# Reordering the input projection's groups in a hybrid decoder trunk, and the sampled convolution as products of all taps

## The chip, the core and the metric

The kernel runs on one core of a Trainium2 chip. The engines named below are TensorE (PE, the matrix engine, with its weight loads), VectorE (DVE), ScalarE (ACT), GpSimd (POOL) and SyncE (SP, which issues most DMAs). Each engine works through its own instruction stream in order and waits on semaphores for the others. The metric is the device time of one execution, in microseconds.

## The reference

A trunk of two layers processes two batches at once: a prompt of 512 tokens, and 8 sampled sequences of 4 tokens each with a paged cache of 2048 earlier positions. Each layer projects 1024 features to 2048, gives them to four mixers of width 256, joins these by an output projection, and ends with a gated feed-forward part. Cut to what the change touches:

```python
h = rms_norm(x, g_mix_pre)
a, ga, u, vb, q, k, v, xd = split(h @ w_in, 8)              # eight groups of 256 columns
# A: causal depthwise convolution, 31 taps; the sampled batch has 30 earlier rows in state_conv
ext = concatenate([prev, a * sigmoid(ga)], axis=1)
ya = silu(layer_norm(conv_general_dilated(ext, w_dw, feature_group_count=256) + b_dw))
# B: chunked spatial gating
v_ = layer_norm(gelu(vb));  yb = gelu(u) * (einsum('gts,bnsgc->bntgc', tril(w_s), v_) + b_s)
# C: differential attention, 4 heads with two softmax maps each;  yc = rms_norm(o, 1e-5) * (1 - lam_init)
# D: causal pooling over 2/4/8/16 rows, minus the token, per-group linear
mix = concatenate([ya, yb, yc, yd], axis=-1) @ w_out
x = x + rms_norm(mix, g_mix_post)
x = x + rms_norm((silu(gate) * up) @ w_down, g_ffn_post)    # gate, up = rms_norm(x, g_ffn_pre) @ w_gu
```

## The kernel before

Features lie on the partitions and tokens along the free axis. Dense products are made as three: each operand is split into a rounded part and a rest (`hi`, `lo`), and hi·hi, lo·hi and hi·lo are summed in PSUM. `whi` and `wlo` are the split weights; the rounding (line 194) is done on ACT, the difference (line 197) on DVE or POOL.

**The input projection.** The list `order` names eight groups of 256 columns: 0 (a), 256 (its gate), 1280 (k), 1024 (q), 1536 (v), 1792 (pooling), 512 (u) and 768 (vb). Each of the groups but v is worked in two blocks of 128 columns; each block first makes a half of 256 columns (tokens 0 to 255) and, two steps later, a half of 288 (the other 256 and the 32 sampled tokens). A half is 24 matmuls into a tile of the pool `acc`, which has two banks of PSUM, given out in program order. ACT copies the results out (lines 374 to 377).

**The flows.** Mixers are Python generators. The loop over steps calls `advance`, which lets each active flow issue one more piece, so that a mixer's instructions are put between the projection's. A flow in `urgent` issues under a high priority. `conv` (31 taps on DVE, then transposes, LayerNorm and tanh), `attention`, `gating` and `pooling` become active when their columns are there; a scheduler then orders each engine's stream by readiness and priority.

**Attention** works in units (i, hh) of a block of 128 queries and a head, for heads 0 and 1 (c = 0) and then 2 and 3 (c = 1). `scores` makes two score tiles `s`, a reduction with bias and minimum on DVE (line 501) and an exp on ACT (line 503); `weights` takes a reciprocal, combines the two maps (lines 513 to 515), transposes (line 518) and copies to `pt` (line 520); `values` fills `oT`. After the last unit the tail (lines 543 to 560) takes squares (`sq`), a power on POOL (line 554), its broadcast `rb`, and makes `yc`.

**Gating** transposes the 128x128 weights `wn` into `wt` (lines 578 to 581), multiplies them with `sgr`, applies gelu to all four parts of `uv` and the sampled columns of `zs` (lines 593, 594), makes `vn` and, at lines 612 and 615, `yb`.

**The output projection** (`project_last`) runs over `W_OUT_TURNS`, four token tiles in two halves each; each turn sums 24 matmuls in the order of `W_OUT_ORDER`, whose entries 0 and 1 are ya, 2 and 3 yb, 4 and 5 yc, 6 and 7 yd. After both halves of a tile `finish` adds the residual, normalizes twice (lines 1300 to 1315, on DVE, ACT and POOL) and turns the result back with PE transposes (`sx`, line 239), which `xlo` and `xhi` (lines 241, 242) split for the feed-forward part.

**The sampled mixers** (`sample`) run beside the output projection. `sample_conv` holds, for 8 sequences, 30 earlier rows and 4 new ones in `ext` (tile `scx`) and adds 31 taps on DVE: two operations at line 883 and sixty at line 886, all 128x32. The sampled attention follows; POOL gathers its pages (`kr`, line 1000).

Of the kernel before, what the change touches and what calls it, by code (L numbers as in the profile page):

```python
# [24 lines left out]
CW = 31  # L25
# [19 lines left out]
W_OUT_ORDER = (6, 7, 0, 1, 2, 3, 4, 5)  # L45
# [77 lines left out]
def trunk(ctx, tc, A, O):  # L123
# [18 lines left out]
    def ps():  # L142
        return psx("ps")
# [210 lines left out]
    def mixing(l, mp, early):  # L354
# [35 lines left out]
        def ev_qk(nm, c, f):  # L390
# [20 lines left out]
            (1536, "v"),  # L411
            (1792, [(14, ev_copy(dext[0], 14, 1.0, 15)), (15, ev_copy(dext[1], 15, 1.0, 15))]),
            (512, [(4, ev_copy(uv[:, 0], 4)), (5, ev_copy(uv[:, 1], 5))]),
            (768, [(6, ev_copy(uv[:, 2], 6)), (7, ev_copy(uv[:, 3], 7))]),
# [17 lines left out]
        convs = []  # L432

        def conv():
            for c in range(2):
                while len(convs) <= c:
                    yield
                yield from convs[c]
            o = ps()
# [128 lines left out]
        def gating():  # L568
# [23 lines left out]
            for f in (2, 0):  # L592
                S.activation(uv[:, f:f + 2], uv[:, f:f + 2], AF.Gelu)
            S.activation(zs[:, 4:8, :], zs[:, 4:8, :], AF.Gelu)
# [10 lines left out]
            for c in range(2):  # L605
                o = acc()
                for n in range(4):
                    for hh in range(2):
# [4 lines left out]
                                       bsg[:, c:c + 1, :].to_broadcast([128, 4, 128]), op0=ALU.mult, op1=ALU.add)  # L613
                tf = uv[:, 2 + c, :]
# [104 lines left out]
        for u in range(n + LAG):  # L719
# [19 lines left out]
            if b >= 0:  # L739
# [9 lines left out]
                if c0 == 256 and i == 0:  # L749
                    convs.append(taps(0))  # L750
                    active.append(conv())
                if c0 == 256 and i == 1:
                    convs.append(taps(1))
# [7 lines left out]
                if i == "v":  # L761
                    done.add("v")
                if c0 == 768 and i == 1:
                    active.append(gating())
                    urgent.append(active[-1])
# [90 lines left out]
    def sample_conv(l, mp, cmn):  # L856
# [25 lines left out]
        for c in range(2):  # L882
            V.tensor_scalar(a[:, c], ext[:, c, :, 0:4], pf[:, 8 + c:9 + c], pf[:, c:c + 1], op0=ALU.mult, op1=ALU.add)
        for t in range(1, CW):
            for c in range(2):
                V.scalar_tensor_tensor(a[:, c], ext[:, c, :, t:t + 4], pf[:, 8 + 2 * t + c:9 + 2 * t + c], a[:, c],  # L886
                                       op0=ALU.mult, op1=ALU.add)
            if t % 4 == 0:
                yield
        o = ps()  # L890
# [18 lines left out]
    def sample(l, sp, share):  # L909
        ys = sp.tile([128, 8, NT], F32, tag="ys", name="ys")  # L910
        hs_in = sp.tile([128, 8, NT], F32, name="hs_in")
        with tc.tile_pool(name=f"smx{l}", bufs=1, reuse_waits="tile") as mp:
            yield
            flows = [sample_conv(l, mp, sp), sample_gate(l, mp, sp), sample_pool(l, mp, sp, PW[l])]
            while flows:
                for fl in list(flows):
                    if next(fl, 0) == 0:
                        flows.remove(fl)
                yield
# [555 lines left out]
```

## Time and profile before

| | |
|---|---|
| median of 3 runs | 1471.88 us (1468.3 to 1475.19) |
| the profiled execution | 1470.1 us |
| its span, first to last instruction | 1468.2 us |
| PE busy | 1393.0 us, 95% |
| DVE, ACT, POOL busy | 816.3, 490.4, 253.9 us |
| mean granted TensorE clock | 0.981 |
| instructions | 22964 |

Busy times come from one profiled execution. The granted clock is the share of full speed that TensorE was given: 1.00 is 2.4 GHz, 0.50 is 1.2 GHz, and a figure between them is a stretch that had both. Matmuls are pipelined, so rows of 0.29 us can start every 0.13 us. What ended an engine's idle time is inferred from semaphore events.

### The profile page before, as it was taken

To read this page: it belongs to the slowest core of one execution; us is meant where nothing else is said; L and a number is where in the kernel's file an instruction comes from. 1 tells how busy PE (TensorE), PEld (TensorE's weight loads), DVE (VectorE), ACT (ScalarE), POOL (GpSimd) and SP (SyncE) were. 2 spreads that over 40 slices of the span, in tenths; PEclk is the share of its full clock that TensorE was granted. 3 is DMA by queue.
4 is the path that set the end of the run, shared out by engine and by line. 5 is a ranking of instruction groups with operands and counts; after the bars stand their busy time and mean duration, and the time that the engine had idled before them with its cause. 6 is when DMAs were issued, how large, how long until landed. Compare 5 with 4: busy or idle time off the path is not lost.

```text
span 1468.2 us, 22964 instructions
## 1 busy us (share of the span) xinstructions
PE 1393.0 (95%) x9274; PEld 1085.7 (74%) x9274; DVE 816.3 (56%) x1624; ACT 490.4 (33%) x972; POOL 253.9 (17%) x271
## 2 busy tenths in 40 slices
PE   6999798989999999999989997989899999999997
PEld 6988677856676777777779886787566677777775
DVE  4997577866424323433669856867564333333344
ACT  4345444322224221222333464433222332222231
POOL 1000245443300000000210004434342000000003
PEclk9999998999999999999999999999999999999999
DMA  6220336786859731323432213378767596213132
GB/s 206 93 87 30 131 117 213 257 299 230 286 177 292 238 137 58 104 69 128 152 115 73 73 53 109 128 244 299 274 235 266 182 299 210 100 58 115 58 133 90
DMA packets 155204, 235.60 MB, mean 160 GB/s; under 512 B 8880, under 2 KB 116410, under 8 KB 155098
## 3 DMA queue, kind: packets, MB, share of 16 engines
q1 hardware_dynamic: 136522, 166.76, 34.8%
q0 software_dynamic: 18432, 67.12, 12.8%
q8 instruction: 73, 1.20, 0.3%
q14 instruction: 33, 0.27, 0.1%
q10 hardware_dynamic: 144, 0.26, 0.0%
HBM read 222.07 MB, written 12.04 MB: 159 GB/s over the span
## 4 chain that ended last, share of the span: by engine, by line
PE 73%; DVE 8%; issue 7%; DMA 6%; POOL 3%; ACT 2%; another core or an unknown queue 0%; SPq 0%; POOLq 0%; DVEq 0%; ACTq 0%
PE acc L128 57%; PE sx L128 8%; DMA kr<-in_cache_k_dram,ik 4%; PE ps L128 2%; PE s L128 2%; DVE sca L886 2%; POOL vr L1030 1%; DVE wlo L197 1%; PE oT L128 1%; POOL kr L1000 1%; DVE m L1315 1%; ACT whi L194 1%; POOL rsw L178 1%; DMA rws<-in_w_gu_dram 1%; PE ps L518 1%
## 5 line engine op out<-in xcount | busy, mean ns | idle before, releaser
L128 PE MATMUL acc<-xhi,whi 128*128 128x512 f32 (+2 forms) x1152 | 409.5, 357 | 3.7 <-issue 1.7
L128 PE MATMUL acc<-xlo,whi 128*128 128x512 f32 (+2 forms) x1152 | 406.7, 353 | 4.2 <-DVE xlo L242 3.2
L128 PE MATMUL acc<-xhi,wlo 128*128 128x512 f32 (+2 forms) x1152 | 407.1, 354 | 0.4 <-issue 0.2
L197 DVE TENSOR_TENSOR wlo<-raw,whi 128x1024 fp32r<-128x1024 f32 x172 | 216.6, 1265 | 198.8 <-ACT whi L194 193.0
L194 ACT CAST whi<-raw 128x1024 fp32r<-128x1024 f32 x178 | 184.3, 1048 | 362.9 <-PE acc L128 320.8
L128 PEld LDWEIGHTS acc<-xhi,whi 128*128 128x128 f32 x1152 | 219.7, 191 | 47.5 <-issue 14.2
L128 PEld LDWEIGHTS acc<-xlo,whi 128*128 128x128 f32 x1152 | 219.9, 191 | 35.8 <-issue 5.7
L128 PEld LDWEIGHTS acc<-xhi,wlo 128*128 128x128 f32 x1152 | 219.6, 191 | 34.6 <-issue 7.9
L128 PE MATMUL acc<-whi,h 128*128 128x512 f32 x704 | 224.7, 396 | 0.6 <-issue 0.6
L128 PEld LDWEIGHTS acc<-whi,h 128*128 128x128 f32 x704 | 131.3, 188 | 44.5 <-issue 11.2
L128 PE MATMUL acc<-wlo,h 128*128 128x512 f32 x352 | 138.4, 395 | 0.0
L1290 POOL TENSOR_TENSOR m<-m,g_g_ffn_post 128x512 f32<-128x512 f32 x14 | 20.2, 1449 | 511.2 <-ACT junk L1289 511.2
L1003 DVE STREAM_TRANSPOSE kt<-kr 128x1024 f32<-128x1024 f32 x64 | 78.3, 1234 | 47.4 <-DMA kr<-in_cache_k_dram,ik 26.9
L1000 POOL DMA_INDIRECT kr<-in_cache_k_dram,ik x64 | 70.3, 1099 | 109.8 <-DVE kt L1003 85.3
L427 DVE SCALAR_TENSOR_TENSOR cacc<-hext,pf,cacc 128x512 f32<-128x512 f32 x120 | 86.9, 745 | 0.8
L128 PEld LDWEIGHTS acc<-wlo,h 128*128 128x128 f32 x352 | 66.1, 188 | 18.0 <-issue 4.6
L1030 POOL DMA_INDIRECT vr<-in_cache_v_dram,iv x64 | 60.5, 945 | 84.7 <-PE sx L128 67.0
L1359 DVE SCALAR_TENSOR_TENSOR th<-th,acc 128x512 f32<-128x512 f32 (+1 forms) x46 | 29.6, 644 | 78.9 <-PE acc L128 78.9
L178 POOL TENSOR_TENSOR rsw<-rsw,mhalf 128x1 f32<-128x1 f32 (+2 forms) x62 | 38.5, 628 | 172.0 <-DVE rsw L177 169.1
L128 PE MATMUL sx<-kt,qs 128*32 128x128 f32 x1024 | 49.3, 278 | 9.3 <-issue 8.6
L554 POOL TENSOR_TENSOR rse<-e,mhalf 128x8 f32<-128x8 f32 x4 | 7.5, 1879 | 257.4 <-DVE e L552 257.4
L1361 ACT CAST h<-th 128x512 fp32r<-128x512 f32 (+1 forms) x48 | 27.9, 582 | 66.5 <-DVE th L1359 58.9
(422 smaller groups left out, 1835.9 us busy)
## 6 DMA issues: line engine op xcount, KB each, us to landing
raw<-in_w_gu_dram SPq DMA_DIRECT2D x44, 1024.0 KB
raw<-in_w_down_dram SPq DMA_DIRECT2D x20, 1024.0 KB
rws<-in_w_gu_dram SPq DMA_DIRECT2D x40, 512.0 KB
raw<-in_w_in_dram SPq DMA_DIRECT2D x16, 1024.0 KB
raw<-in_w_out_dram SPq DMA_DIRECT2D x8, 1024.0 KB
rwo<-in_w_out_dram SPq DMA_DIRECT2D x16, 512.0 KB
rws<-in_w_down_dram SPq DMA_DIRECT2D x16, 512.0 KB
x<-x_t SPq DMA_DIRECT2D x12, 512.0 KB
```

The source lines that it names most:

```text
L128: T.matmul(out, lhsT, rhs, start=start, stop=stop)
L178: G.tensor_tensor(y, v, mhalf[:P, :n], op=ALU.pow)
L194: S.copy(hi, src)
L197: eng.tensor_tensor(lo, src, hi.bitcast(F32), op=ALU.subtract)
L427: V.scalar_tensor_tensor(a, hext[c][:, t:t + SEQ], pf[:, 8 + 2 * t + c:9 + 2 * t + c], a, op0=ALU.mult, op1=ALU.add)
L886: V.scalar_tensor_tensor(a[:, c], ext[:, c, :, t:t + 4], pf[:, 8 + 2 * t + c:9 + 2 * t + c], a[:, c], op0=ALU.mult, op1=ALU.add)
L1000: G.indirect_dma_start(out=kr, out_offset=None, in_=ck, in_offset=bass.IndirectOffsetOnAxis(ap=ik[:, s, bg:bg + 1], axis=0))
L1003: V.transpose(kt, kr)
L1030: G.indirect_dma_start(out=v.rearrange("p t e -> p (t e)"), out_offset=None, in_=cv, in_offset=bass.IndirectOffsetOnAxis(ap=iv[:, s, a:a + ...
L1290: (V if (t, half) == (3, 1) else G).tensor_tensor(m[t][:, hs], m[t][:, hs], gain[:, hs], op=ALU.mult)
L1359: V.scalar_tensor_tensor(th[:, :n], th[:, :n], 0.5, ou[:, :n], op0=ALU.mult, op1=ALU.mult)
L1361: S.copy(hh, th[:, :n])
```

## The change

Five edits, as the diff shows. In the input projection vb comes before the pooling columns and u. The gelu is split: the half for vb is issued early, the half for u when u is done; the flow of the gating starts after vb. The order of the output projection's parts is yc, ya, yd, yb. The convolution's flow becomes urgent after its taps. The sampled convolution makes, for each half of the channels and of the sequences, one product of all 31 taps (4 sequences x 4 tokens x 31) and one sum over the taps; the bias is added afterwards. The three sampled flows issue under the high priority.

```diff
-W_OUT_ORDER = (6, 7, 0, 1, 2, 3, 4, 5)
+W_OUT_ORDER = (4, 5, 0, 1, 6, 7, 2, 3)
...
             (1536, "v"),
+            (768, [(6, ev_copy(uv[:, 2], 6)), (7, ev_copy(uv[:, 3], 7))]),
             (1792, [(14, ev_copy(dext[0], 14, 1.0, 15)), (15, ev_copy(dext[1], 15, 1.0, 15))]),
             (512, [(4, ev_copy(uv[:, 0], 4)), (5, ev_copy(uv[:, 1], 5))]),
-            (768, [(6, ev_copy(uv[:, 2], 6)), (7, ev_copy(uv[:, 3], 7))]),
...
                 yield from convs[c]
+            urgent.append(flow["conv"])
+            yield
...
-            for f in (2, 0):
-                S.activation(uv[:, f:f + 2], uv[:, f:f + 2], AF.Gelu)
-            S.activation(zs[:, 4:8, :], zs[:, 4:8, :], AF.Gelu)
+            S.activation(uv[:, 2:4], uv[:, 2:4], AF.Gelu)
+            S.activation(zs[:, 6:8, :], zs[:, 6:8, :], AF.Gelu)
...
+                yield
+            while "u" not in done:
+                yield
+            S.activation(uv[:, 0:2], uv[:, 0:2], AF.Gelu)
+            S.activation(zs[:, 4:6, :], zs[:, 4:6, :], AF.Gelu)
+            for c in range(2):
                 tf = uv[:, 2 + c, :]
...
+                if c0 == 512 and i == 1:
+                    done.add("u")
...
         for c in range(2):
-            V.tensor_scalar(a[:, c], ext[:, c, :, 0:4], pf[:, 8 + c:9 + c], pf[:, c:c + 1], op0=ALU.mult, op1=ALU.add)
-        for t in range(1, CW):
-            for c in range(2):
-                V.scalar_tensor_tensor(a[:, c], ext[:, c, :, t:t + 4], pf[:, 8 + 2 * t + c:9 + 2 * t + c], a[:, c],
-                                       op0=ALU.mult, op1=ALU.add)
-            if t % 4 == 0:
-                yield
+            k = pf[:, 8 + c:9 + c]
+            taps_ = bass.AP(k.tensor, k.offset, [k.ap[0], (0, 4), (0, 4), (2, CW)])
+            for hf in range(2):
+                e = ext[:, c, 4 * hf:4 * hf + 4]
+                win = bass.AP(e.tensor, e.offset, [e.ap[0], (34, 4), (1, 4), (1, CW)])
+                pr = cmn.tile([128, 512], F32, tag="pr", bufs=2, name="sct")[:, :16 * CW].rearrange("p (s t j) -> p s t j", s=4, t=4)
+                V.tensor_tensor(pr, win, taps_, op=ALU.mult)
+                V.tensor_reduce(a[:, c, 4 * hf:4 * hf + 4], pr, axis=AX, op=ALU.add)
+                yield
+            V.tensor_scalar(a[:, c], a[:, c], pf[:, c:c + 1], None, op0=ALU.add)
...
-                for fl in list(flows):
-                    if next(fl, 0) == 0:
-                        flows.remove(fl)
+                with tc.high_priority(URG):
+                    for fl in list(flows):
+                        if next(fl, 0) == 0:
+                            flows.remove(fl)
```

The diff alone doesn't tell what stands where. On **PE, in the second half of attention of layer 0**, this stood in a row before (`s` are scores, `oT` values, `ps<-cst,p` transposes of the weights, and `acc<-xhi,whi` and its two companions the projection; the last figures are the shape):

```order
L128 MATMUL s<-k1h,q1l 128x384
L128 MATMUL oT<-pt,vtok 64x128
L518 MATMUL ps<-cst,p 128x128 x2
L128 MATMUL oT<-pt,vtok 64x128
L518 MATMUL ps<-cst,p 128x128 x2
L128 MATMUL acc<-xhi,whi 128x288
L128 MATMUL acc<-xlo,whi 128x288
L128 MATMUL acc<-xhi,wlo 128x288
```

After the last scores with 384 columns shown here came the values and transposes of one unit and then a half of the projection. Of the changed kernel, this is the end of the same attention:

```order
L128 MATMUL oT<-pt,vtok 64x128 x9
L521 MATMUL ps<-cst,p 128x128 x8
L128 MATMUL oT<-pt,vtok 64x128 x8
L128 MATMUL ps<-cst,sq 128x2 x4
L128 MATMUL ps<-cst,rb 128x128
L444 MATMUL ps<-cst,hext_233 30x128
L453 MATMUL ps<-cst,cacc_466 128x128
L444 MATMUL ps<-cst,hext_234 30x128
L453 MATMUL ps<-cst,cacc_827 128x128
L128 MATMUL ps<-cst,rb 128x128 x3
L581 MATMUL acc<-cst,wn 128x128 x4
```

The values, `sq` and `rb` of the tail, and the transposes of the convolution follow each other, and the gating's `wn` comes behind the last `rb`. After three more of the convolution's transposes PE has:

```order
L453 MATMUL ps<-cst,cacc_827 128x128
L128 MATMUL acc<-wt,sgr 64x128 x4
L128 MATMUL acc<-xhi,whi 128x256
L128 MATMUL acc<-xlo,whi 128x256
L128 MATMUL acc<-xhi,wlo 128x256
```

The three last rows here are the first of the projection since the 256-wide scores at the start of this half of attention; all six remaining halves of the projection follow from there.

On **ACT, in the same stretch**, between the exps (`p,den<-p,mn`) with 256 and 384 columns, before:

```order
L376 ACTIVATE dext_236<-acc 128x256
L377 ACTIVATE zs<-acc 128x32
L503 ACTIVATE p,den<-p,mn 128x256 x2
L374 ACTIVATE uv<-acc 128x256
L503 ACTIVATE p,den<-p,mn 128x384
L520 COPY pt<-ps 128x128 x2
L503 ACTIVATE p,den<-p,mn 128x384
```

and now, with line 506 the exp, 595 the gelu of vb and 596 its sampled columns:

```order
L376 ACTIVATE uv<-acc 128x256
L377 ACTIVATE zs<-acc 128x32
L506 ACTIVATE p,den<-p,mn 128x256
L595 ACT_TABLE_LOAD
L595 ACTIVATE uv<-uv 128x1024
L596 ACTIVATE zs<-zs 128x64
L506 ACT_TABLE_LOAD
L506 ACTIVATE p,den<-p,mn 128x256
L506 ACTIVATE p,den<-p,mn 128x384 x4
```

The gelu and two loads of ACT's function table stand between the two exps of the second unit with 256 columns.

On **DVE, in the finish of the output projection of layer 0**, before (`x_t` and `m` are links of the finish of the first tile, `sumt` and `rsw` its sums):

```order
L1308 SCALAR_TENSOR_TENSOR x_t<-m_2038,rsw,x_t 128x1024
L886 SCALAR_TENSOR_TENSOR sca<-scx,pf_84,sca 128x32 x8
L177 TENSOR_SCALAR rsw<-sumt 128x1
L886 SCALAR_TENSOR_TENSOR sca<-scx,pf_84,sca 128x32 x5
L1315 SCALAR_TENSOR_TENSOR m_2038<-x_t,rsw,g_g_ffn_pre 128x1024
L886 SCALAR_TENSOR_TENSOR sca<-scx,pf_84,sca 128x32 x2
L1300 TENSOR_TENSOR sumt<-sumt 128x1
L886 SCALAR_TENSOR_TENSOR sca<-scx,pf_84,sca 128x32 x2
```

and now, at the finish of the last tile, with line 901 the product and 902 the sum:

```order
L1324 SCALAR_TENSOR_TENSOR x_t<-m_2042,rsw,x_t 128x1024
L242 TENSOR_TENSOR xlo<-sx,xhi 128x4x128
L901 TENSOR_TENSOR sct<-scx,pf_84 128x496
L177 TENSOR_SCALAR rsw<-sumt 128x1
L901 TENSOR_TENSOR sct<-scx,pf_84 128x496
L902 TENSOR_REDUCE sca<-sct 128x16
L1374 SCALAR_TENSOR_TENSOR th<-th,acc 128x256
L1331 SCALAR_TENSOR_TENSOR m_2042<-x_t,rsw,g_g_ffn_pre 128x1024
L902 TENSOR_REDUCE sca<-sct 128x16
```

The small operations are gone from the finishes of the first tiles; the products begin in that of the last one.

## Rows read from the trace of the kernel before

**Rows 1.** The page, part 1: busy time of each engine, share of the span, instructions.
```profile
PE 1393.0 (95%) x9274; PEld 1085.7 (74%) x9274; DVE 816.3 (56%) x1624; ACT 490.4 (33%) x972; POOL 253.9 (17%) x271
```

**Rows 2.** Slices, layer 0: length, busy us and count per engine, PEclk, DMA share, GB/s.
```profile
130.00:140.00 10.00, 9.91 (x63) 7.10 (x62) 8.47 (x21) 6.62 (x18) 0.00 (x0) 1.00 0.00 1
...
160.00:170.00 10.00, 6.59 (x41) 4.28 (x39) 8.25 (x29) 3.43 (x7) 4.26 (x7) 0.98 0.67 235
170.00:180.00 10.00, 7.68 (x44) 5.83 (x44) 4.99 (x13) 1.07 (x2) 1.84 (x4) 0.68 0.08 16
...
220.00:230.00 10.00, 6.84 (x25) 5.72 (x26) 10.00 (x25) 4.36 (x8) 5.88 (x6) 0.66 0.27 83
...
240.00:250.00 10.00, 7.37 (x49) 6.90 (x48) 6.25 (x14) 4.00 (x11) 5.52 (x7) 0.83 0.56 184
```

**Rows 3.** PE's waits, 140 to 250 us: total, times, longest.
```profile
PE sx L239 <- DVE m L1315: 5.1, 3, 2.6
PE sx L239 <- DVE xlo L242: 3.4, 1, 3.4
PE acc L128 <- ACT yb L351: 2.7, 1, 2.7
...
PE acc L600 <- DVE bsg L590: 0.5, 1, 0.5
```

**Rows 4.** Timeline of PE: start, us, operation, count [idle before <-releaser].
```profile
147.23 1.43 PE L128 MATMUL oT<-pt,vtok 128*64 128x128 f32 x16
...
151.08 0.30 PE L128 MATMUL acc<-xhi,whi 128*128 128x288 f32 x1
151.22 0.29 PE L128 MATMUL acc<-xlo,whi 128*128 128x288 f32 x1
...
180.90 0.50 PE L128 MATMUL acc<-whi,yb 128*128 128x512 f32 x1 [2.71 <-ACT yb L351]
```

**Rows 5.** Timeline of ACT, 146 to 190 us.
```profile
148.97 0.56 ACT L543 COPY os__1608<-oT 128x512 f32<-128x512 f32 x1
149.55 1.28 ACT L593 ACT_TABLE_LOAD   x1
150.84 1.06 ACT L593 ACTIVATE uv<-uv 128x1024 f32<-128x1024 f32 x1
...
167.01 1.44 ACT L460 ACTIVATE cacc<-ps,pf 128x512 f32<-128x512 f32 x2 [4.46 <-PE ps L458]
168.35 1.14 ACT L461 ACTIVATE hext<-cacc 128x512 f32<-128x512 f32 x2
```

**Rows 6.** ACT by line, 117.2 to 148.7 us: busy, mean ns | idle before.
```profile
L503 ACT ACTIVATE p<-p,mn 128x256 f32<-128x256 f32 (+2 forms) x12 | 7.4, 616 | 5.9 <-DVE mn L501 5.9
```

**Rows 7.** DVE by line, 117.2 to 146 us.
```profile
L501 DVE CUSTOM_DVE_ANT_0 p<-s,pb 128x256 f32<-128x256 f32 (+2 forms) x12 | 6.3, 554 | 2.0 <-PE s L128 2.0
L515 DVE SCALAR_TENSOR_TENSOR p<-p,den 128x128 f32<-128x128 f32 (+3 forms) x8 | 4.0, 547 | 0.1
...
L655 DVE SCALAR_TENSOR_TENSOR wn<-wn,cst,dext 128x497 f32<-128x497 f32 x1 | 0.7, 731 | 0.0
```

**Rows 8.** Timeline of POOL, 146 to 190 us.
```profile
155.18 1.64 POOL L554 TENSOR_TENSOR rse<-e,mhalf 128x8 f32<-128x8 f32 x1 [32.04 <-DVE e L552]
```

**Rows 9.** DVE by line, 195 to 250 us, then 920 to 980 us.
```profile
L886 DVE SCALAR_TENSOR_TENSOR sca<-scx,pf,sca 128x32 f32<-128x32 f32 x60 | 18.5, 366 | 0.0
...
L886 DVE SCALAR_TENSOR_TENSOR sca<-scx,pf,sca 128x32 f32<-128x32 f32 x60 | 17.5, 349 | 0.0
```

**Rows 10.** Timelines of DVE and of POOL, 204 to 250 us.
```profile
218.94 3.56 DVE L886 SCALAR_TENSOR_TENSOR sca<-scx,pf,sca 128x32 f32<-128x32 f32 x2
...
220.11 2.34 POOL L197 TENSOR_TENSOR wlo<-raw,whi 128x1024 fp32r<-128x1024 f32 x1
```

**Rows 11.** Slices of 20 us in layer 1.
```profile
940.00:960.00 20.00, 17.19 (x89) 14.49 (x88) 19.53 (x46) 10.83 (x24) 11.47 (x11) 0.87 0.43 134
960.00:980.00 20.00, 17.55 (x142) 17.01 (x140) 10.26 (x21) 6.10 (x16) 10.10 (x14) 0.96 0.72 256
```

More of the change, by code (lines that the diff above doesn't have):

```diff
@@ L432, in mixing @@
         convs = []
+        flow = {}
         def conv():
@@ L751, in mixing @@
                     active.append(conv())
+                    flow["conv"] = active[-1]
                 if c0 == 256 and i == 1:
```

## The prediction

> **What bounds the kernel now.** I read the page's busy line first: TensorE (PE) works 1393.0 us of a span of 1468.2 [rows 1], so only some 75 us of idle PE time, and what a lower clock costs, can be won, and whatever makes PE stand still is lost at full price. Next I read the slices for the layer's two loose places, then PE's waits there. Place one is the input projection and the start of the output projection: while attention runs, its scores and transposes are threaded through the projection's dense matmuls and PE is busy 9.91 of 10 us (the slices from 130 to 140) [rows 2]. PE stops only afterwards, when the mixers' tails come in one by one: 6.59 and 7.68 of 10, the second at a granted clock of 0.68 (the slices from 160 to 180) [rows 2]. Six waits named there add to 7.5 us, the longest 2.7 for yb, the shortest 0.5 [rows 3]. Place two is the end of the output projection: 6.84 at clock 0.66 and 7.37 at 0.83 (the slices from 220 to 250) [rows 2]; the waits there are for the finish chain on VectorE (DVE), 5.1 us for m and 3.4 for xlo [rows 3]. The second layer repeats both in other sizes.
>
> The profiled execution took 1470.1 us, 1.9 outside the span; the median of the three runs is 1471.88. I sum against 1470.1 and don't correct for the other 1.8. About 0.5%, some 7 us, is what a measurement of this kernel can tell from no change.
>
> **Part 1: the projection's order and the gating.** The words say that a group is moved; the order of PE's instructions says more. The gating flow now starts when vb is done, and takes both banks of "acc", for the transposes of wn and for wt·sgr, before the remaining six half-blocks ask for theirs; on PE those two stand behind the last transposes of attention. So from 117 us on PE gets the whole rest of attention without one dense matmul between, then the gating's weights, and only then the six half-blocks. Before, the same six were the filler.
>
> What attention alone takes I walk link by link. Twelve score reductions (6.3 us) and eight weight steps (4.0) lie on DVE [rows 7], twelve exps of 0.62 on ScalarE (ACT) [rows 6], with transposes and copies between. On ACT the split gelu now stands between two exps of one unit: a table load of 1.28 us, the gelu of 1.06, a small one of about 0.2, and a load of 1.28 back to exp [rows 5]: 3.8 us in which the reciprocal on DVE, and the score reduction behind it, wait. With these I get the last exp at about 138, the last weights at 140.5, and the values done at 143.2; before, amid dense work, at 148.66 (147.23 + 1.43) [rows 4].
>
> Then comes a tail in single file: seven operations of 128x512 on ACT, DVE and POOL (copy, square, rb, os, the yc cast, wt and its mask) at about 0.6 [rows 5], 4.3 us; e and the pow on POOL, 0.2 + 1.64 [rows 8]; some 36 small matmuls at 0.09 (16 took 1.43 [rows 4]), 3.2. That is 9.3, with hand-overs 10.5. The first dense matmul of the six half-blocks starts at 153.7.
>
> After it PE has 25 us up to the end of the projection: 96 matmuls of 288 columns at 0.133 (the step of two starts [rows 4]) and 48 of 256 columns at 0.12, 18.5; 48 small ones for uv, xn and wt·vn, 4.3; pooling and the first yc products, 2. That ends at 178.7. There ACT has, in a row, the block's evacuation (0.6), the conv affines once xn is turned (1.44), a table load (1.28), the gelu of u (1.06 + 0.2), two tanh (1.14) [rows 5], then wn, yd and ya at some 0.6. ya is ready 8.7 us after the last block, and PE has 3.6 us of yc, xn and pooling to cover that: 5.1 us idle, and 0.5 more behind it. Twenty-four matmuls of the output projection are done at 190.2. Before, they were done at 180.9, where yb is released [rows 4]. **Cost at full clock: 9.3 us a layer, 18.6 in two.** As a cross-check: the new idle time, 20.7 us, takes the place of 7.5 idle [rows 3] and 2.5 of slow clock (0.32 of 7.68 [rows 2]), 10.7; I keep the walk's. It could be 4 us less a layer, if the table loads fall into slack and hand-overs are short, or as much more.
>
> **The clock.** After the gaps of 160 to 170 the granted clock was 0.68, and the slices at 6.84 and 7.37 busy are at 0.66 and 0.83 [rows 2]; each fall goes with a slice at 6.6 to 7.7 of 10. In my walk PE is busy only 4 to 6 of 10 between 121 and 153, so half clock is likely there; what it costs is bounded by PE's own links in the chain (6.5 us), the restart (3) and the end gap (3), less the dip already counted: 0 to 8 us a layer. I take 5, **10 in two layers**, because most links are on DVE and ACT. The Trainium skill, TensorE: Matmul & The Clock Gate, Part 1 on the HAM clock gate, says that PE's clock is lowered by how busy PE has lately been, which speaks against this change; the falls above agree, and by it alone the upper end, 1490, would come out (the first half of rival (c)).
>
> On the table load the trace shows a copy from 148.97 for 0.56, the load from 149.55 for 1.28 and the gelu at 150.84 [rows 5]: nothing but the load lies between. The Trainium skill, ScalarE: Activation LUTs, What ACT_TABLE_LOAD costs, adds a drain of about 1.38 us to every switch; by it the two extra switches of a layer would make the sum some 5.5 us higher, an estimate from that page, and this trace doesn't agree with it.
>
> **Part 2: the output projection's order, conv urgent.** The order is now yc, ya, yd, yb. yc is ready first; yb, the last before with 2.7 of wait [rows 3], is last again and comes out of the same row of ACT and DVE steps as ya. I book nothing beyond the end gap above.
>
> **Part 3: the sampled convolution.** Sixty-two small DVE operations go; the sixty of line 886 cost 18.5 us in layer 0 and 17.5 in layer 1 [rows 9], where a few last far longer than the rest: two took 3.56 us, beside POOL's wlo of 2.34 [rows 10]. They stand between the links of the finish chain, where PE waits for m and xlo. Added are four products of 128x496 and four sums a layer. The nearest row for a product is the 128x497 operation at 0.73 [rows 7]; a sum, which no row shows, reads as much from one input: between half a product and a whole one, I take 0.6. Eight are about 5 us, behind most of the chain and beside dense matmuls; a product and a sum come ahead of the last m, about 1 us.
>
> Place two loses in layer 0 the waits of 5.1 and 3.4 [rows 3] and, as missing clock times busy time, 0.34 x 6.84 + 0.17 x 7.37 = 3.6 [rows 2]: 12.1. In layer 1 it is idle 2.81 + 2.45 and clock 2.2 + 0.7, 8.2 [rows 11]. The last turn has nothing but its chain, and its wait (the longest of the three for m was 2.6 [rows 3]) stays. **I take 10 and 6, together −16**; the bounds are −8 (the xlo wait and part of the clock, in layer 0 and the like in layer 1) and −20.3 (all).
>
> **Part 4: priority and the gathers.** The sampled LayerNorm now comes after the products, and POOL's first gather of kr stands behind it, by order some 6 us later in the stage. The sampled attention is fed by DMA and has slack in places. I take +1 in two layers, between −10 and +10.
>
> **The sum.** 1470.1 + 18.6 + 10 − 16 + 1 = 1483.7: **1484 us**.
>
> **The rivals.**
> (a) Clock kept, the two places cancel. The gaps in attention are many and short, and PE keeps its clock: 1470.1 + 18.6 − 16 + 1 = 1474, no difference. For it: the falls here came with single waits of 1 to 3 us, not with a fine mix. Against: nothing in the trace shows PE at half load for 30 us at full clock. Chance 0.22.
> (b) Faster: the finish chain decides. Attention without dense matmuls ahead of its scores is bound by DVE alone (6.3 + 4.0 and small change), the table loads fall into time in which ACT waits for score reductions (5.9 us in this stretch [rows 6]), the chain is 4 us shorter a layer, and place two gives all it has: 1470.1 + 2 x 5.3 − 20.3 = 1460. It decides if the six half-blocks start before about 149. Against: the next DVE step needs the exp behind the gelu. Chance 0.18.
> (c) The clock at its worst, 1470.1 + 18.6 + 16 − 16 + 1 = 1490, and with gathers too late 1499. For it: the low slices above. Against: few PE links are in the chain. Chance 0.10.
> (d) The change doesn't do what it says: the split gelu brings yb no earlier, and the end gap is yb's in place of ya's, the same 5 us. That lies inside the forecast.
>
> **How the numbers follow.** The forecast (1479 to 1489) has 0.50, the others as given. The range goes from a little under (b) to (c): 1459 to 1498. Faster by over 0.5% is (b) and a little of (a), 0.20; within 0.5% 0.22; slower 0.58.
>
> **What would show it.** In the profile after: PE busy 4 to 6 of 10 from 121 to 153, no projection matmul between the scores, three table loads ahead of the output projection, the first 256-column block after attention near 154, an end gap of about 5 us for ya near 182; at place two no 128x32 operation in the finish and waits of 2 to 4 us. I am wrong if the slices in attention stay above 8 of 10, if the blocks start before 149, or if place two still waits over 6 us a layer.

## The result, and the profile after

The changed kernel takes 1510.09 us (median of four runs, 1503.62 to 1513.12) against 1472.68 of the kernel before on the same chip: a ratio of 1.0251, 95% interval 1.021 to 1.0293. It is slower, as forecast, but by 37 us where the forecast said some 14, and beyond the range's end of 1498.

The profiled execution of after took 1503.62 us with a span of 1501.9, 33.7 more than that of before. Its page, part 1, answers to [rows 1]:

```profile
PE 1416.8 (94%) x9274; PEld 1098.4 (73%) x9274; DVE 804.7 (54%) x1520; ACT 499.5 (33%) x978; POOL 259.0 (17%) x271
```

PE has as many instructions as before, 23.8 us more busy time and 9.9 more idle time. So most of the loss is not standing still: it is matmuls at a lower clock, or matmuls whose counted times overlap less. Where it lies is read from four stretches of each kernel: from 115 us to the start of the last turn (line 239) of the output projection in layer 0, then the sampled attention up to its last `kt,qs` matmul (`kt,qs` are its scores, `vr,pt` its values), and the same two in layer 1. The columns are those of [rows 2]. Before:

```profile
115.00:243.30 128.30, 111.58 (x689) 90.88 (x688) 95.13 (x263) 63.52 (x141) 38.55 (x40) 0.95 0.33 110
243.30:390.10 146.80, 139.97 (x1235) 104.11 (x1235) 94.53 (x197) 41.48 (x75) 64.30 (x63) 0.97 0.78 272
854.60:966.90 112.30, 100.07 (x585) 81.25 (x585) 79.78 (x205) 54.41 (x117) 36.38 (x38) 0.94 0.35 114
966.90:1117.70 150.80, 139.56 (x1234) 103.59 (x1234) 94.36 (x197) 42.41 (x76) 62.58 (x63) 0.98 0.76 270
```

After:

```profile
115.00:253.80 138.80, 114.86 (x682) 94.14 (x680) 85.83 (x198) 66.31 (x139) 41.71 (x40) 0.91 0.30 102
253.80:408.70 154.90, 145.54 (x1247) 108.22 (x1247) 98.11 (x205) 41.12 (x75) 62.28 (x63) 0.97 0.77 263
869.90:998.00 128.10, 111.54 (x616) 90.48 (x615) 73.80 (x152) 55.51 (x116) 38.97 (x38) 0.86 0.30 99
998.00:1158.90 160.90, 154.44 (x1286) 111.71 (x1286) 99.83 (x208) 44.02 (x78) 63.97 (x63) 0.99 0.71 256
```

The first stretch is 10.5 us longer in layer 0 and 15.8 in layer 1. Missing clock times length goes from 6.4 to 12.5 us in layer 0 and from 6.7 to 17.9 in layer 1, idle time from 16.7 to 23.9 and from 12.2 to 16.6. The sampled attention is 8.1 and 10.1 us longer; the two dense stretches behind it, up to layer 1 and up to the end, give 3.3 and 7.5 back. Together 10.5 + 15.8 + 8.1 + 10.1 - 3.3 - 7.5 = 33.7.

**Stage one** in slices of 10 us; the last two are layer 1:

```profile
120.00:130.00 10.00, 6.50 (x33) 5.11 (x32) 5.62 (x20) 8.20 (x20) 1.66 (x1) 0.72 0.32 107
130.00:140.00 10.00, 8.37 (x53) 5.02 (x53) 7.09 (x19) 5.55 (x16) 0.00 (x0) 0.93 0.00 1
140.00:150.00 10.00, 5.77 (x41) 4.86 (x41) 0.59 (x2) 2.66 (x5) 1.64 (x1) 0.75 0.09 27
...
160.00:170.00 10.00, 6.10 (x36) 5.42 (x34) 6.62 (x16) 1.80 (x4) 2.04 (x2) 0.83 0.00 0
...
870.00:880.00 10.00, 10.00 (x35) 5.76 (x34) 5.92 (x17) 4.98 (x14) 0.00 (x0) 0.50 0.01 2
880.00:890.00 10.00, 8.99 (x49) 6.16 (x48) 2.84 (x9) 3.32 (x8) 0.00 (x0) 0.55 0.00 0
```

Where PE had been 9.91 of 10 busy [rows 2], attention now runs at 6.50, 8.37 and 5.77. In layer 1 the same order ran at half clock for most of 20 us; the 10.00 there is not full work but small matmuls that last twice as long. PE's waits from 117 to 262 us, which answer to [rows 3]:

```profile
PE acc L128 <- ACT ya L351: 4.6, 1, 4.6
PE s L128 <- DVE mn L504: 3.5, 2, 3.1
PE sx L239 <- DVE m L1331: 3.5, 2, 2.4
PE ps L128 <- DVE rb L559: 2.6, 1, 2.6
PE acc L128 <- DVE vn L604: 2.5, 1, 2.5
...
PE acc L128 <- POOL wt L584: 1.1, 1, 1.1
```

The wait for yb and that for xlo are gone, and the waits for m fall from 5.1 to 3.5. New are the links of attention (mn, rb). The waits for the gating's `wt` and `vn` and for ya stood before at 0.7, 1.4 and 1.2 us and are 1.1, 2.5 and 4.6 now. PE's timeline at four of these places, with columns as in [rows 4]:

```profile
153.55 0.39 PE L128 MATMUL acc<-xhi,whi 128*128 128x256 f32 x1
...
161.97 0.44 PE L602 MATMUL acc<-cst,uv 128*128 128x128 f32 x2 [1.15 <-ACT zs L377]
164.90 0.35 PE L128 MATMUL acc<-xhi,whi 128*128 128x256 f32 x1 [2.49 <-DVE vn L604]
...
166.49 0.41 PE L128 MATMUL acc<-xhi,whi 128*128 128x256 f32 x1
166.71 0.41 PE L128 MATMUL acc<-xlo,whi 128*128 128x256 f32 x1
...
185.74 0.29 PE L128 MATMUL acc<-xhi,wlo 128*128 128x288 f32 x1
...
194.04 0.79 PE L128 MATMUL acc<-whi,ya 128*128 128x512 f32 x1 [4.62 <-ACT ya L351]
```

The six half-blocks start at 153.55 and end at 186.0, with a step of 0.21 instead of 0.12 from 165.4 to 168.7. The output projection waits for ya until 194.04. What PE waited for at 164.90 is seen on DVE:

```profile
161.54 0.15 DVE L177 TENSOR_SCALAR rsw<-ag 128x1 f32<-128x1 f32 x1
161.62 1.22 DVE L197 TENSOR_TENSOR wlo<-raw,whi 128x1024 fp32r<-128x1024 f32 x1
162.87 0.70 DVE L645 TENSOR_TENSOR s<-dext 64x526 f32<-64x526 f32 x1
163.61 0.69 DVE L645 TENSOR_TENSOR wn<-dext 64x512 f32<-64x512 f32 x1
164.22 0.53 DVE L604 TENSOR_SCALAR vn<-acc,ag,rsw 128x256 f32<-128x256 f32 x1
```

`vn`, the gating's LayerNorm, reads a bank of `acc` that the next half-block wants. It sends `rsw` to POOL for a power (1.49 us there, from 161.77), and in DVE's order a weight split and two pooling steps stand ahead of it. So a step of 0.53 begins 2.6 us after the first of these three (161.62 to 164.22), with the bank held.

**Place two.** The products and the sums, layer 0, in the columns of [rows 7]:

```profile
L901 DVE TENSOR_TENSOR sct<-scx,pf 128x496 f32<-128x496 f32 x4 | 2.7, 671 | 0.4 <-DMA out_dram<-cn 0.4
L902 DVE TENSOR_REDUCE sca<-sct 128x16 f32<-128x496 f32 x4 | 2.7, 664 | 0.0
```

They cost 5.4 us in place of the 18.5 of [rows 9]; a sum costs as much as a product. The products use the two buffers in which the sampled convolution's state goes out to DRAM (`cn`), and waited 0.4 us for that. They start as the last turn is near, and the sampled attention's first gather comes behind them: 10.2 us after the last turn (263.92 against 253.76), where before it came 2.2 us after (245.55 against 243.30). In layer 1 it is 14.4 against 2.2.

### The profile page after: what moved, and what is told of

Its sections match the earlier page's. It is cut to its first block, busy times and chain, and to the rows that moved or that the text cites. A ratio compares the mean times of both kernels' runs of the same rounds, so it can differ in the third digit from the quotient of the medians.

```text
span 1501.9 us, 22894 instructions
## 1 busy us (share of the span) xinstructions
PE 1416.8 (94%) x9274; PEld 1098.4 (73%) x9274; DVE 804.7 (54%) x1520; ACT 499.5 (33%) x978; POOL 259.0 (17%) x271
## 4 chain that ended last, share of the span: by engine, by line
PE 77%; issue 7%; DVE 5%; ACT 4%; DMA 3%; POOL 2%; another core or an unknown queue 1%; SPq 0%; POOLq 0%; DVEq 0%; ACTq 0%
PE acc L128 58%; PE sx L128 9%; PE ps L128 3%; PE s L128 2%; DMA kr<-in_cache_k_dram,ik 1%; DVE wlo L197 1%; ACT whi L194 1%; PE oT L128 1%; PE ps L521 1%; POOL kr L1016 1%; DVE kt L1019 1%; PE ps L239 1%; DVE x_t L1324 1%; POOL vr L1046 1%
## 5 line engine op out<-in xcount | busy, mean ns | idle before, releaser
L128 PEld LDWEIGHTS acc<-wlo,h 128*128 128x128 f32 x352 | 66.1, 188 | 19.2 <-issue 5.9
L128 PE MATMUL sx<-vr,pt 128*32 128x256 f32 x512 | 57.4, 387 | 1.4 <-issue 1.4
L128 PEld LDWEIGHTS sx<-kt,qs 128*32 128x32 f32 x1024 | 33.6, 110 | 26.0 <-issue 19.9
```

The source lines that it names most:

```text
L128: T.matmul(out, lhsT, rhs, start=start, stop=stop)
```

## The experiments

Five series, each on one chip with the kernel before beside it. The chips differ: the kernel before took 1442 us in series 1 (one chip), 1440 in series 2 and 5 (a second) and 1464 and 1465 in series 3 and 4 (a third). Ratios are to the kernel before of the same series. The expectations of series 1 count from the 1472.7 of the result, so they compare by ratio too. For short, W is the new order of `W_OUT_ORDER`, C the urgent convolution, A the projection's groups with the split gelu and the early gating, S the products, P the priority of the sampled flows.

### Series 1: which part costs

**Everything but A.**

```diff
-            (768, [(6, ev_copy(uv[:, 2], 6)), (7, ev_copy(uv[:, 3], 7))]),
             (1792, ...
             (512, ...
+            (768, [(6, ev_copy(uv[:, 2], 6)), (7, ev_copy(uv[:, 3], 7))]),
...
+            for f in (2, 0):
+                S.activation(uv[:, f:f + 2], uv[:, f:f + 2], AF.Gelu)
```

> The changed kernel with the projection's groups, the gelu and the gating's start as before; the other four edits stay. Theory 1 (the early gating takes both acc banks and its transposes stand behind attention, so PE runs attention without the projection; this is worth 18.7 us in layer 0 and 22.8 in layer 1 of the profiled run): the loss goes, what place two gains (7.5 + 6.9) stays, less the 7.3 us that the later gathers cost: 1472.7 - 14.4 + 7.3 = about 1465, between 1458 and 1470. Rival A (the loss is the sampled part's priority and late gathers): 1490 or more. Rival B (the output projection's order or the urgent convolution makes the end gap): 1480 to 1490.

Measured: 1445.28 us, 1.003 (1.0008 to 1.0052), where Theory 1's 1465 of 1472.7 is 0.995: the loss goes, but the gain of the rest isn't there. **A alone**, in the kernel before:

> The kernel before with the first edit alone: vb ahead of the pooling columns and u, the gelu split, the gating started after vb. Theory 1: the whole loss of stage one and nothing of the gains: 1472.7 + 18.7 + 22.8 = 1514, between 1505 and 1520. Rival A: 1475 to 1485. Rival B: the end gap is smaller with yd and ya first, 1490 to 1500.

Measured: 1476.15 us, 1.0233 (1.019 to 1.0276), +34 us, inside Theory 1's range by ratio (1.022 to 1.032). So nearly all of the loss is A's. Its slice from 130 to 140 has a clock of 0.50 and its wait for `vn` is again 2.5 us.

**The gating's two tiles from another pool.** The transposes of `wn` and `wt·sgr` no longer take the banks of `acc`:

```diff
-            o = acc()
+            o = ps()
```

(at both places; the rest as in after)

> The changed kernel, but the gating's first two PSUM tiles (the transposes of wn and wt.sgr) come from the pool ps with three banks instead of acc with two. By order the remaining halves of the projection then stand between attention's scores again; the gelu and the two table loads stay between the exps. Theory 1: PE is above 9 of 10 busy in attention again, the six halves start near 121 and the time falls by 30 us or more, to 1460 to 1478. Rival C (the two table loads inside attention are the loss, PE only waits for them): PE still stands for 3 us or more in each layer's attention, several times, and the time stays above 1490.

Measured: 1462.17 us, 1.0145 (1.0106 to 1.0183). After, in series 2 on another chip, is at 1.0352, so two names of a pool are worth some 30 us (0.0207 of 1441), as Theory 1 had it. But its upper end, 1478, is a ratio of 1.004, and the kernel stays above that. The slices, to be held against those of after:

```profile
120.00:130.00 10.00, 9.38 (x70) 8.19 (x70) 6.44 (x21) 7.73 (x19) 2.21 (x2) 1.00 0.29 105
...
140.00:150.00 10.00, 9.69 (x66) 9.09 (x66) 6.26 (x19) 2.91 (x8) 1.10 (x2) 0.79 0.01 2
150.00:160.00 10.00, 5.46 (x42) 4.66 (x42) 3.83 (x6) 3.11 (x6) 2.09 (x1) 0.90 0.41 131
```

Four of the six half-blocks are back in attention: two among the scores (9.38 at full clock), two behind the last scores. The other two still stand behind the tail (5.46).

**Products and priority alone** (S and P in the kernel before):

> The kernel before with the sampled convolution as products and sums and the sampled flows with priority; projection, gating, convolution and the output projection's order as before. Theory 1 with the terms of the two traces: 1472.7 - 14.4 + 7.3 = about 1465. Rival A: slower than before, 1478 or more, through later gathers. If the gain at place two needs the other order of the output projection, the same as before, 1472.

Measured: 1453.54 us, 1.0093 (1.006 to 1.0126). The part that was to gain 15 us lost 11.5.

### Series 2: both kernels on one chip, and the parts apart

The kernel before, and after:

> The kernel before, unchanged, for a trace on the chip of these runs. If this is the chip of the first four, about 1442; against its own earlier trace (1470) every theory expects the input projection to read the same, and the difference in the sampled attention and the feed-forward part, where PE's waits for issue and DMA are.

> The changed kernel, unchanged, beside the parts: ratio 1.02 to 1.03 to the kernel before. If the parts add up as in the first four runs (first edit alone +34, sampled edits alone +11, all but the first edit +3), +34 + 3 = +37; if the later gathers hide behind the later projection, less.

Measured: 1443.43 us in the traced run (median of the series 1439.8), and 1492.14 us, 1.0352 (1.0307 to 1.0397), above the 1.02 to 1.03 expected. After has a mean clock of 0.963 here; in layer 0 its first stretch takes 147.0 us at 0.83, against 138.8 at 0.91 in the result.

**The products alone**, without priority:

> The kernel before with the sampled convolution as products and sums alone, without the priority. Theory 2 (the priority lets the sampled flows push the finish chain and the gathers back; the products themselves only relieve DVE): faster than before by 5 to 14 us. Rival D (the products and sums are late by themselves, since DVE makes them behind the finish, and the gathers with them): slower than before by 5 to 12 us, as with the priority.

Measured: 1460.27 us, 1.0144 (1.0107 to 1.0182). **W and C alone:**

> The kernel before with only the output projection's new order and the urgent convolution. From the first four runs (all but the first edit 1445, sampled edits alone 1453) these two are worth about -8: 0.994 of before if they stand for themselves (the end gap before yb is covered); 1.00 if they only repair what the sampled edits cost.

Measured: 1432.17 us (eight runs), 0.9944 (0.9925 to 0.9963): faster than both kernels. Of the change, the two edits at which I booked nothing are the ones that gain. Which of the two does it was not separated.

### Series 3: the rest of A, and the products earlier

**The gating's tiles from ps and the gelu in one piece after u**, so that no table load stands in attention:

```diff
-            S.activation(uv[:, 2:4], uv[:, 2:4], AF.Gelu)
-            S.activation(zs[:, 6:8, :], zs[:, 6:8, :], AF.Gelu)
+            while "u" not in done:
+                yield
+            S.activation(uv, uv, AF.Gelu)
+            S.activation(zs[:, 4:8, :], zs[:, 4:8, :], AF.Gelu)
```

> The changed kernel with the gating's first two tiles from the pool ps (as in the run before with that one edit, 1462) and the gelu in one piece after u, so that the gelu and its table loads are out of attention. If the two loads between the exps are what was left of the loss there (17 us against the kernel with the old groups, 1445): 1443 to 1450. If the tail in which wn and wt.sgr stand behind attention's last transposes is what was left: 1456 or more.

Measured: 1489.61 us, 1.0197 (1.0145 to 1.0248), no better than with the split gelu. Attention is whole again (PE 10.00, 10.00 and 9.48 of 10 from 120 to 150, at full clock), but the wait has moved:

```profile
170.00:180.00 10.00, 4.46 (x18) 1.91 (x17) 7.83 (x28) 4.21 (x7) 3.18 (x6) 0.78 0.11 28
```

The whole gating chain now stands behind the projection with nothing to cover it (4.46). So to take the table loads out of attention did not win back what remained of A's cost. What the loads cost by themselves isn't shown, since the gating's chain moved with them.

**The groups' new order alone**, gelu and gating as before, after u:

> The kernel before with only the order of the groups changed (vb, pooling, u); the gating starts after u, the gelu is in one piece. Theory 1 (not the groups' order but the gating's early start costs): within 5 us of before, 1435 to 1445. Rival F (the pooling's sums on DVE, now later and beside attention's end, cost by themselves): 1450 or more.

Measured: 1470.87 us, 1.0057 (1.0026 to 1.0088). With vb first and nothing of it used early, the order costs 7 to 8 us, between the two expectations.

**The products ahead of the state's write-out**, S alone and with W and C:

```diff
-        (the write-out of the state through cn)
         for c in range(2):
             ... (products, sums, bias)
+        (the write-out of the state through cn)
```

> The kernel before with the sampled convolution as products and sums, but made ahead of the write-out of the convolution's state, which goes to the end of the flow. The products' buffers are of the ring pr (two buffers) that the write-out also uses; by order they now stand between the second and the third turn. Theory 3 (in the change the products wait for the write-out's buffers and DMAs, come after the finish, and POOL's gathers come 10 to 14 us later after the last turn): the gathers start no later than 2.2 us after the last turn, as before, and the time falls to 1440 - 6.4 - 5.5 = about 1428, 1424 to 1434. Rival D (products and sums are slower by themselves): 1450 or more, as with the first form (1460).

> The same with the output projection's new order and the urgent convolution. If the gains add: 1440 - 7.6 - 12 = about 1420, and faster than both kernels; if they are the same gain (the finish's waits), 1428 to 1432.

Measured: 1475.11 us, 1.0074 (1.0042 to 1.0105), and 1467.31 us, 1.0027 (0.9999 to 1.0054). In the first of the two the gathers come early again, 1.2 and 1.6 us after the last turn in the two layers, but the last turn of layer 0 stands at 243.4 (241.1 in the kernel before on that chip): the products are now between the second and third turn, in the finish chain. These two forms have the early gather or the short finish, not both.

Theory 3's time falls with the first of the two runs: its gathers come earlier than before's 2.2 us in both layers, and it is 11 us slower. The early gather does go with a shorter sampled attention: 145.6 and 154.1 us in the two layers, against 173.7 and 162.9 with the products in their first form on that chip (series 4). But the kernel before has 151.8 and 146.0 there, so layer 1 is 8 us longer with an earlier gather. Lateness is a part of the loss, not the whole.

### Series 4: the wait for gsub

> The kernel before, unchanged, for a trace on the chip of this call: the first gather of kr 2.2 us after the last turn, and no wait of DVE for gsub, as in its two earlier traces.

> The kernel before with the sampled convolution as products and sums alone, once more, beside the next run. If the earlier figure holds on this chip too, 1.014 of before; the first gather of kr 12 us after the last turn in layer 0.

Measured: 1471.01 us in the traced run, and for the products alone 1482.2 us, 1.0112 (1.0073 to 1.0151). With products DVE waited for a load of `gsub` ahead of the sampled attention, up to 8.8 us in one piece here and 10.1 in series 2. **The scale of gsub folded into its use:**

```diff
-        V.tensor_scalar(gsub, gsub, 1.0 - lam_init, None, op0=ALU.mult)
...
-        V.tensor_tensor(ov, ov, gsub.unsqueeze(1).to_broadcast([NT, 4, 64]), op=ALU.mult)
+        V.scalar_tensor_tensor(ov, ov, 1.0 - (0.8 - 0.6 * math.exp(-0.3 * l)), gsub.unsqueeze(1).to_broadcast([NT, 4, 64]), op0=ALU.mult, op1=ALU.mult)
```

> The same, but DVE's scaling of gsub at the start of the sampled attention (the first reader of a load of 8 KB that SP issues after the flows are done) is folded into the multiplication that uses gsub at its end. Theory 4 (the late flows put that load among the gathers' traffic, and DVE, in order, stood 10.1 and 4.9 us before it, with the key transposes, wlo and the feed-forward's sums behind): no wait for gsub, 10 to 15 us faster than the run beside it, so within 5 us of before or faster. Rival G (the lateness of the gathers themselves costs, the wait only covers it): within 4 us of the run beside it.

Measured: 1482.88 us, 1.0114 (1.007 to 1.0158), the same as without the edit. That explanation falls. With W and C:

> As the run before, with the output projection's new order and the urgent convolution, which alone gave 0.9944. Theory 4: 0.985 to 0.992 of before. Rival G: 1.000 to 1.006.

Measured: 1455.45 us, 0.9934 (0.9916 to 0.9952), faster than both kernels by ratio, and between the ranges of Theory 4 and of Rival G.

### Series 5: what the products are worth

Two kernels with W, C and the folded gsub, the second with the products:

> The kernel before with the new order of the output projection, the urgent convolution and the scale of gsub folded into its use, taps one by one as before. Theory one (in this surrounding the product form of the sampled convolution pays at place two and costs it back in the sampled attention, nothing is left over): ratio 0.992 to 0.996, within 0.3% of the same kernel with products. Theory two (the product form itself gains the 10 us of place two once the gathers come early): this one stays at 0.994 to 0.997 and the one with products is 0.4% or more below it. Theory three (the products cost 8 us a layer whatever stands around them): this one is 0.985 to 0.99, clearly below the one with products.

> The same with the taps as products, for comparison on one chip. Theory one: ratio 0.992 to 0.996, as the one without products within 0.3%. Theory two: 0.99 or below on a chip with little wait for gathers, 0.4% or more below the one without products. Theory three: 0.993 or above and 0.4% or more above the one without products. In all three the last finish of layer 0 is some 8 us ahead of the kernel before, and by theories one and three the sampled attention after it is longer by about as much.

Measured: 1432.43 us, 0.9942 (0.9924 to 0.996), and 1436.55 us, 0.9968 (0.9954 to 0.9983). The products add some 0.3%, at the limit of what these runs tell apart: they give back what they gain. Three stretches of each (115 us to the last turn, to the last `kt,qs`, to layer 1), first without:

```profile
115.00:237.40 122.40, 112.08 (x682) 90.87 (x681) 94.15 (x258) 63.30 (x140) 40.28 (x40) 0.94 0.35 115
237.40:371.20 133.80, 131.92 (x1235) 100.46 (x1236) 94.63 (x196) 41.47 (x75) 64.58 (x63) 1.00 0.83 295
371.20:735.70 364.50, 359.39 (x2059) 269.30 (x2059) 148.47 (x220) 104.04 (x177) 23.64 (x29) 0.99 0.47 155
```

and with products:

```profile
115.00:231.80 116.80, 108.25 (x686) 88.07 (x685) 83.94 (x204) 64.31 (x142) 41.32 (x40) 0.99 0.37 121
231.80:379.10 147.30, 144.89 (x1269) 109.77 (x1273) 98.06 (x203) 41.40 (x75) 65.21 (x63) 0.99 0.80 283
379.10:738.30 359.20, 354.27 (x2030) 263.04 (x2030) 148.28 (x220) 103.74 (x176) 23.64 (x29) 1.00 0.47 151
```

The stretch up to the last turn is 5.6 us shorter, with the clock up from 0.94 to 0.99; the sampled attention is 13.5 longer, and 5.3 of it comes back: +2.6 in layer 0, and by the same reading of layer 1 about +2.5. PE is not idle in the longer stretch (2.4 us against 1.9). Part of what it holds is work that came earlier: matmuls of the feed-forward part's last product (`h`), 15 without and 44 with products, 7.7 us more of PE (columns PE, PEld, DVE, ACT, clock, DMA share, GB/s):

```profile
237.40:371.20 133.80, 3.65 (x15) 2.74 (x15) 5.67 (x10) 5.34 (x10) 1.00 0.83 295
```

```profile
231.80:379.10 147.30, 11.35 (x44) 8.02 (x44) 5.66 (x10) 4.91 (x9) 0.99 0.80 283
```

The rest is spread. A row that seems to name it is the busy time of the sampled attention's values in the whole execution, without products, with them, and in series 3 with the products ahead of the write-out:

```profile
L128 PE MATMUL sx<-vr,pt 128*32 128x256 f32 x512 | 46.5, 383 | 0.7 <-DMA vr<-in_cache_v_dram,iv 0.7
```

```profile
L128 PE MATMUL sx<-vr,pt 128*32 128x256 f32 x512 | 56.0, 384 | 1.0 <-DMA vr<-in_cache_v_dram,iv 1.0
```

```profile
L128 PE MATMUL sx<-vr,pt 128*32 128x256 f32 x512 | 55.2, 385 | 3.0 <-DMA vr<-in_cache_v_dram,iv 2.7 <-issue 0.3
```

The same 512 matmuls of the same mean duration cover 9.5 us more. But that is no loss of 9.5, as PE's timeline of the kernel with products shows:

```profile
300.01 0.40 PE L128 MATMUL sx<-vr,pt 128*32 128x256 f32 x1
300.03 0.42 PE L128 MATMUL sx<-kt,qs 128*32 128x128 f32 x6
```

A values matmul alone between `kt,qs` counts 0.40, though the next matmul starts 0.02 later; 26 in a row count 1.91, so that each adds 0.06. By the time from one start to the next, the values take 14.1 us in the longer stretch against 12.4, and `kt,qs` 21.9 against 19.2. The same row of before and after on the result's chip reads 43.2 and 57.4.

Nor does the pattern need late gathers: in the run with early ones the row still reads 55.2. The pattern goes with the kernel, not with the chip: the values of a layer stand in 26 groups in all three traces of the kernel before, and in 45 (layer 0) and 44 (layer 1) in both traces of after. So it is an order in PE's instruction stream. The thirteen traces with products read 54.4 to 57.6 us in this row, the seven without 43.2 to 47.8; what the order costs was not tested alone.

## Why the prediction was wrong in size

**Right in kind, in part by luck.** Part 1 decides, and the walk up to its middle held in layer 0: the values were put at 143.2 and are done at 142.3, the first half-block was put at 153.7 and came at 153.55, and no projection matmul stands between the scores. But it held for that layer alone. From the same row, the last 14 values matmuls of the first half of attention, to the first half-block it is 38.2 us in layer 0 and 42.8 in layer 1:

```profile
115.39 1.09 PE L128 MATMUL oT<-pt,vtok 128*64 128x128 f32 x14
...
858.24 1.09 PE L128 MATMUL oT<-pt,vtok 128*64 128x128 f32 x14
...
901.07 0.39 PE L128 MATMUL acc<-xhi,whi 128*128 128x256 f32 x1
```

In the two layers of after in series 2 it is 44.7 and 43.0. The sign "PE busy 4 to 6 of 10" failed as well: 6.5, 8.4 and 5.8 in layer 0, 10.0 and 9.0 at half clock in layer 1. The end gap for ya was put at 5.1 and is 4.62 by luck: the ACT steps listed for it add to 7.5 us, not 8.7, unless the 1.14 that both tanh take together is counted twice, and a weight split that stood ahead of them isn't in the list:

```profile
185.93 1.05 ACT L194 CAST whi<-raw 128x1024 fp32r<-128x1024 f32 x1 [2.51 <-PE acc L128]
...
191.11 1.13 ACT L464 ACTIVATE hext<-cacc 128x512 f32<-128x512 f32 x2
```

Rival (b) needed a start before 149 and fell. Rival (a) needed the clock to hold, and it did not. (c) comes nearest with 1499, but lacks the waits below. Of (d), the end gap is ya's, as the forecast had it.

**The step that failed first: "PE has 25 us up to the end of the projection".** It took 32.4 (153.55 to 186.0), and as much in layer 1. I counted the 48 small matmuls for uv, xn and wt·vn at their issue time alone. They take turns with the half-blocks in the two banks of `acc` (a ring: each tile takes the next bank in program order), and each waits for what reads the bank: 1.2 for `zs`, 2.5 for `vn`, five more of 0.25 to 0.46, together 5.4 us; the matmuls that ran at half clock after that wait add 1.5. Twenty-four matmuls of the output projection were done at 198.9, not 190.2: 7 us from this step, the rest from the restart at half clock behind the gap for ya.

The run with the gating's tiles from the other pool shows that the tiles' place in the ring is the cause of the larger part of A's cost: some 30 of the 49 us that A costs within the whole change (1492.14 against 1445.28, on two chips, read through the two series' kernels before). In its layer 0 the waits in the ring are 1.8 us in place of 5.4. It also puts four half-blocks back into attention, which the forecast had priced; so the 5.4 by itself is read from the trace, not tested.

**The clock cost in sum about what I took beyond the walk, but not where I took it.** I took 5 us a layer. Beside the 1.5 behind `vn`, twelve matmuls behind the gap for ya ran at a step of 0.43 where full clock gives 0.23, some 2. In layer 1 the half clock in attention adds 4.7. That is some 3.6 and 8.3 us, an estimate from these rows. Within the walk of layer 0 a lower clock is hidden too: eight `rb` matmuls took 2.08 us there, 1.16 in layer 1 of the kernel before. The same order of instructions ran at 0.72 to 0.93 in the attention of layer 0, at 0.50 and 0.55 in layer 1, at 0.50 in layer 0 of after in series 2 and, with A alone, at 0.50 in one slice of layer 0. My bound of 8 rested on PE's own links in the chain; in layer 1 PE is counted busy 10.00 of 10 at half clock, so that the other matmuls became links too. The Trainium skill, TensorE: Matmul & The Clock Gate, Part 1 on the HAM clock gate, says that the clock follows how busy PE has lately been; the trace agrees in kind, as full clock before attention (1.00 from 100 to 120) falls to 0.72 where PE is busy 6.50 of 10.

Stage one as a whole: 18.75 us in layer 0 and 22.8 in layer 1, measured at the twenty-fourth matmul of the output projection, against 14.3 each. That is 13 of the 20 us by which the terms fall short (33.7 against 13.6).

**The small terms.** The two extra table loads cost 1.28 each, as taken: the exp's last step started at 120.95 for 0.20, the load at 121.17:

```profile
120.95 0.20 ACT L506 ACTIVATION_READ_ACCUMULATOR p<-p,mn 128x1 f32 x1
121.17 1.28 ACT L595 ACT_TABLE_LOAD   x1
```

The drain that the Trainium skill, ScalarE: Activation LUTs, What ACT_TABLE_LOAD costs, adds isn't here either. Place two gave 14.4 us (7.5 and 6.9) where 10 and 6 were taken, close to it.

**Priority and gathers: +1 taken, +7.3 measured** for all that stands behind the last turns. The bounds were right, the value was not. I saw from the order that the first gather would move and set a price near nothing because the sampled attention "has slack in places". The two stretches grew by 18 us, of which 11 came back. The first gather came 8 us later against the last turn in layer 0 and 12 in layer 1. By series 3 that is a part of the loss; no run moved the gathers alone, and the rest of the cause stays open. I had also missed that the products share two buffers with the write-out of the state.

The sum by measured terms: -0.75 + 18.75 + 22.8 - 14.4 + 7.3 = 33.7. The first term is the start: at 115.39 the kernel after stands 0.75 us ahead of the kernel before (116.14 for the same row), and the 18.75 counts from there.

**What stays open.** In series 2 the whole change costs more (52 us) than A alone and the rest alone together in series 1 (34 and 3). W and C take 7.6 us off the kernel before, and 27 off the one with products and folded gsub on another chip (1482.88 to 1455.45). And why the sampled attention is longer with products was found in part only.

## What to carry to other kernels

Before work is moved into a small ring of PSUM banks that a dense stream uses, walk the ring: each tile in turn, who reads it, and what stands ahead of that reader on its engine; an issue time is not a price there. Filler between the links of a long chain is worth its cover and the clock of everything around it, so the chain should be priced at half clock as well. Where a finish is made shorter, look at what the freed engine does first, and read the stretch behind it too: here it gave back half of the gain (7.3 of 14.4), and in series 5 all of it.

## What the runs showed of the hardware

- The kernel before took 1442, 1440 and 1465 us on three chips and 1472.7 in the result. Its sampled attention of layer 0, fed by gathers, took 146.8 us there and 136.2 and 151.8 in series 2 and 4, at the same order of instructions; gains of this size compare on one chip only.
- A sum over 31 taps to 128x16 costs what the product of 128x496 does, 0.664 against 0.671 us.
- A busy share of 10.00 can hide a loss: at a granted clock of 0.50 (870 to 880 us) small matmuls fill the time.
- Busy time of a row of small matmuls is no price: alone among others a 256-column matmul counts 0.40, though the next one starts 0.02 later, and in a row each adds 0.06.
